# Square sums chained on VectorE, rows made k-tile by k-tile on ScalarE, and adaLN units loaded later: a hybrid decoder layer

## The chip, the core and the metric

One core of a Trainium2 chip runs the whole layer. The metric is the device time of one execution in microseconds, taken as the median of several runs. In the profile PE is TensorE (matrix products and transposes), ACT is ScalarE, DVE is VectorE, POOL is GpSimd, and SP (SyncE) issues the loads of the weights.

## What is computed

A layer on 256 tokens of width 1024, in fp32: a SwiGLU feed-forward part (ffn1), a token mixer (a causal pooling mixer and a dilated attention, from one input projection), and a second feed-forward part (ffn2). Each is preceded by an RMS norm whose result is scaled and shifted by vectors that are computed from a conditioning vector c (adaLN), and each result is multiplied by a gate vector from c and added to the running h.

```python
def rmsnorm(x, g):
    y = xf * lax.rsqrt(jnp.mean(xf * xf, axis=-1, keepdims=True) + EPS)
    return y * g
mod = silu(c) @ w_ada + b_ada                 # nine vectors of 1024
sh1, sc1, gt1, sh2, sc2, gt2, sh3, sc3, gt3 = split(mod, 9)
n = rmsnorm(h, g_ffn1) * (1 + sc1) + sh1
h = h + 0.5 * gt1 * swiglu(n, w1_gate, w1_up, w1_down)
n = rmsnorm(h, g_mix) * (1 + sc2) + sh2       # norm b
h = h + gt2 * hybrid_mixer(n, w_in, w_pool, pool_scale, w_out)
n = rmsnorm(h, g_ffn2) * (1 + sc3) + sh3      # norm c
h = h + 0.5 * gt3 * swiglu(n, w2_gate, w2_up, w2_down)
return rmsnorm(h, g_final)
```

## The kernel before

**Tiles and products.** The 256 tokens are two row tiles, t = 0 and t = 1, of 128 rows each. A width of 1024 is eight k-tiles of 128 columns. Every fp32 operand of a large product is split into a rounded part and a rest (nh and nl of an activation, hi and lo of a weight), and `gemm` adds three products, nh x hi, nl x hi and nh x lo, of 512 columns each, into a PSUM bank.

**Weights and adaLN.** Weights come through SP's queue as units of 1 MB, in the order that `plan` writes down, into four buffers (`raw`). A unit of weights is cast on ACT (hi, line 266) and subtracted on DVE (lo, line 267), in two halves of 1024 columns. A unit of kind `ada` is instead reduced on DVE by two operations of 1024 columns (line 255), which give two columns of `mod`. The function `weave` inserts these units among the weights; for the mixer the constant `WMIX` (line 42) says after which of its units they come. A buffer is loaded again when the DVE operations that read it are done.

**Order.** The tile scheduler orders every engine's instructions by priority and readiness. `urgent()` raises the priority of what stands in it, and `casts_after` with `behind` adds order dependencies that keep casts of later units behind given instructions.

**The norms between the stages.** Norm b lies between ffn1 and the mixer, norm c between the mixer's output projection (`wout`) and ffn2. For each row tile, `finish1` or `finish2` runs:
- `residual` (line 361): on DVE, two products of the accumulator and the gate row (line 364) and two sums into h (line 366), 512 columns each;
- `rstd` (line 289): two squares with a row sum on ACT (line 294); POOL adds the epsilon (line 296), adds both sums (line 298) and takes the power -1/2 (line 300);
- `norm_rows` (line 314): ACT multiplies both halves of the row by it (line 319, xs);
- later in PE's program, `norm_mod` (line 322): for each half PE transposes four blocks into PSUM (`turn`, line 307, xtb or xtc); then n32 = xs^T x scale + shift, per k-tile, on ACT for half 0 (line 336) and DVE for half 1 (line 338); then ACT casts 512 columns to nh (line 285) and DVE subtracts 512 columns to nl (line 286). In norm c the second half is only copied, and its k-tiles are finished one by one in ffn2.

**Where the turns stand.** Row tile 0's turn of norm b stands among the last four chunks of ffn1's second product for row tile 1, ahead of chunk number `TURN` (line 475). Row tile 1's turn stands in the mixer's second projection of row tile 0, ahead of k-tile 1 of `z["k0"]` (line 731); the turn of q0's heads stands at k-tile 3 there. The scores of the attention (`scores`) take a minimum on DVE (line 667), an exponential on ACT (line 669) and a scaling on DVE (line 673); `heads_out` transposes the probabilities on PE (line 681, pt), copies them on ACT (line 684, pts) and multiplies by the values on PE (line 690).

## Time and profile before

| | |
|---|---|
| median of 3 runs | 494.17 us (493.03 to 494.2) |
| the profiled execution | 494.21 us |
| span of its instructions | 492.4 us, so 1.8 us lie around it |
| mean granted TensorE clock | 0.993 |
| PE busy | 479.4 us (97%) |
| DVE busy | 354.8 us (72%) |
| ACT busy | 260.0 us (53%) |
| POOL busy | 15.6 us (3%) |

The profile gives one execution. A timeline row has the start, the duration and the instruction; in brackets stands how long its engine was idle before it, and what ended that. A row marked x4 groups four instructions. A matmul's start is the useful number, since matmuls overlap: at full clock one of 512 columns starts every 0.227 us. A window row gives, for a stretch, its length and each engine's busy time and count (PE, PE's weight loads, DVE, ACT, POOL), then the granted clock as a share of 2.4 GHz, the share of DMA time and GB/s.

### The profile page before, as it was taken

The page shows a single profiled execution, that of the slowest core. Times are in us where ns is not written, and L with a number is a line of the kernel's source. Part 1 is how long each engine was busy: PE and PEld are TensorE (multiplying, and loading weights), DVE is VectorE, ACT ScalarE, POOL GpSimd, SP SyncE. Part 2 cuts the span into 40 slices and gives each one's busy share as a digit, 9 for nine tenths or more (in the row PEclk, how much of TensorE's full clock was granted, in tenths as well). Part 3 has the DMA queues.
Part 4 walks back from the last instruction along what each step waited for, and adds up shares of the span by engine and source line. Part 5 has one row for each costly group of instructions (what it writes and reads, how often), then busy time and mean ns, then how long its engine had stood idle before and what let it go on. Part 6 is the DMA issues. An engine that isn't in the chain of part 4 may idle for free.

```text
span 492.4 us, 5990 instructions
## 1 busy us (share of the span) xinstructions
PE 479.4 (97%) x2176; PEld 385.1 (78%) x2176; DVE 354.8 (72%) x569; ACT 260.0 (53%) x437; POOL 15.6 (3%) x26
## 2 busy tenths in 40 slices
PE   8999999999999999899999999999999999999994
PEld 5778888888888887778767888888878888888883
DVE  5978989996897896787868776755666756655244
ACT  4776575553544354574677468945543443544121
POOL 1000000000000002120000012000000000000000
PEclk9999999999999999899999999999999999999998
DMA  8999995997987995859775848285367749540002
GB/s 306 400 359 315 369 338 203 369 425 281 396 325 286 338 385 193 309 198 405 317 244 184 298 154 318 106 321 197 126 236 253 281 189 341 180 162 9 35 2 85
DMA packets 20383, 126.05 MB, mean 256 GB/s; under 512 B 2409, under 2 KB 4225, under 8 KB 6018
## 3 DMA queue, kind: packets, MB, share of 16 engines
q1 hardware_dynamic: 17568, 121.25, 65.0%
q10 hardware_dynamic: 2786, 4.43, 2.6%
q8 instruction: 17, 0.28, 0.2%
q14 instruction: 12, 0.10, 0.1%
HBM read 124.61 MB, written 1.06 MB: 255 GB/s over the span
## 4 chain that ended last, share of the span: by engine, by line
PE 87%; DMA 5%; DVE 2%; ACT 2%; POOL 2%; issue 2%; POOLq 0%; DVEq 0%; ACTq 0%
PE accf L411 22%; PE gu L370 9%; PE le L445 9%; PE gu L371 9%; PE gu L372 9%; PE ld L445 6%; PE accm L762 5%; DMA raw<-in_w_dram 4%; PE zp L370 3%; PE zp L372 3%; PE zp L371 3%; PE ht L397 2%; DMA h<-in_x_dram 1%; ACT hi L266 1%; PE sh L370 1%
## 5 line engine op out<-in xcount | busy, mean ns | idle before, releaser
L267 DVE TENSOR_TENSOR lo<-raw,hi 128x1024 fp32r<-128x1024 f32 (+1 forms) x156 | 184.4, 1208 | 45.4 <-ACT hi L266 37.0
L266 ACT CAST hi<-raw 128x1024 fp32r<-128x1024 f32 (+1 forms) x156 | 158.3, 1041 | 78.9 <-PE accf L411 24.9
L255 DVE CUSTOM_DVE_ANT_0 raw<-raw,cb,vecs 128x1024 f32<-128x1024 f32 x70 | 88.1, 1279 | 4.8 <-DMA raw<-in_w_dram 4.8
L411 PE MATMUL accf<-hi,hh 128*128 128x512 f32 x176 | 56.3, 396 | 0.2
L411 PE MATMUL accf<-lo,hh 128*128 128x512 f32 x176 | 56.3, 394 | 0.0
L411 PE MATMUL accf<-hi,hl 128*128 128x512 f32 x176 | 55.7, 390 | 0.0
L370 PE MATMUL gu<-hi,nhc 128*128 128x512 f32 x112 | 44.4, 397 | 0.0
L372 PE MATMUL gu<-lo,nhc 128*128 128x512 f32 x112 | 43.7, 390 | 0.0
L371 PE MATMUL gu<-hi,nlc 128*128 128x512 f32 x112 | 43.7, 390 | 0.0
L388 ACT ACTIVATE sg<-gu 128x256 f32<-128x256 f32 x24 | 9.1, 381 | 65.2 <-PE gu L372 65.2
L411 PEld LDWEIGHTS accf<-hi,hl 128*128 128x128 f32 x176 | 33.0, 188 | 7.4 <-DVE hl L286 0.6
L411 PEld LDWEIGHTS accf<-lo,hh 128*128 128x128 f32 x176 | 33.3, 189 | 6.9
L411 PEld LDWEIGHTS accf<-hi,hh 128*128 128x128 f32 x176 | 32.7, 189 | 7.3 <-ACT hh L285 1.1
L391 DVE TENSOR_TENSOR pr<-sg,gu 128x256 f32<-128x256 f32 x24 | 10.0, 418 | 33.8 <-ACT sg L388 33.8
L370 PE MATMUL gu<-hi,nha 128*128 128x512 f32 x80 | 31.8, 397 | 0.0
L371 PE MATMUL gu<-hi,nla 128*128 128x512 f32 x80 | 31.2, 390 | 0.0
L372 PE MATMUL gu<-lo,nha 128*128 128x512 f32 x80 | 31.2, 390 | 0.0
L370 PE MATMUL zp<-hi,nhb 128*128 128x512 f32 x64 | 26.5, 416 | 0.0
L285 ACT CAST hh<-ht 128x256 fp32r<-128x256 f32 x44 | 14.1, 379 | 21.9 <-PE ht L397 21.9
L372 PE MATMUL zp<-lo,nhb 128*128 128x512 f32 x64 | 25.3, 395 | 0.0
L371 PE MATMUL zp<-hi,nlb 128*128 128x512 f32 x64 | 25.3, 395 | 0.0
L372 PEld LDWEIGHTS gu<-lo,nhc 128*128 128x128 f32 x112 | 21.0, 188 | 4.6
(172 smaller groups left out, 715.1 us busy)
## 6 DMA issues: line engine op xcount, KB each, us to landing
raw<-in_w_dram SPq DMA_DIRECT2D x112, 1024.0 KB, 5.1
raw<-in_w_dram SPq DMA_DIRECT2D x4, 512.0 KB, 7.7
gt<-gd ACTq DMA_DIRECT2D x3, 512.0 KB, 5.4
h<-in_x_dram SPq DMA_DIRECT2D x2, 512.0 KB
bias<-in_bias_dram ACTq DMA_DIRECT2D x4, 256.0 KB, 4.1
out_dram<-o SPq DMA_DIRECT2D x4, 160.0 KB, 2.1
bands<-in_band_dram ACTq DMA_DIRECT2D x4, 136.0 KB, 7.5
gfb<-in_gf_dram ACTq DMA_DIRECT2D x1, 512.0 KB, 4.8
```

Of the source, the lines that this page charges most:

```text
L255: note(nc.vector.tensor_tensor_reduce(r, r, cb, 1.0, vecs[:, m:m + 1], ALU.mult, ALU.add, mod[:, m:m + 1]), i, 1)
L266: note(nc.scalar.copy(hi[:, o:o + n], src), i + s / 2, 0)
L267: note(nc.vector.tensor_tensor(lo[:, o:o + n], src, hi[:, o:o + n].bitcast(F32), ALU.subtract), i + s / 2, 0)
L285: nc.scalar.copy(hi_ap, src)
L370: mm(ps, nh[:, k, :], whi, start=first, stop=False)
L371: mm(ps, nl[:, k, :], whi, start=False, stop=False)
L372: mm(ps, nh[:, k, :], wlo, start=False, stop=last)
L391: nc.vector.tensor_tensor(pr, sg, ps[:, 256:512], ALU.mult)
L397: nc.tensor.transpose(pt[:, i, :], pr[:, ts(i, P)], ident)
L411: mm(accs[b], a[:, k, :], cols(ww, 2 * k + b), start=st, stop=sp)
L445: mm(banks[ci][t], n[t][a][:, j, :], cols(ww, lead_set(f, j).index(ci)), start=j == 0 and p == 0, stop=last and p == 2)
L762: mm(acc2[t][b], a[:, k, :], cols(ww, 2 * kk + b), start=st, stop=sp)
```

## The change

`rstd` and `residual` are taken into `norm_rows`. The row's square sum is now two chained `tensor_tensor_reduce` on DVE, of which the first starts from the epsilon and the second from the first one's sum; POOL only takes the power. ACT makes half 0 of the scaled row and DVE half 1. In `norm_mod`, ACT makes both nh and n32 straight from PSUM, k-tile by k-tile, for both halves, and DVE subtracts two k-tiles at a time. `in_order` fixes the order of these on each engine, and `line_up` fixes in which order the rows, the casts of certain weight units and the k-tile operations come. `TURN` goes from 2 to 3, so that row tile 0's turn stands later in ffn1's chunks by program order; `AFTER1` moves row tile 1's turn from k-tile 1 to k-tile 3 of `z["k0"]`, and q0's heads turn at k-tile 5. `WMIX` loads the eight adaLN units of the mixer stage four weight units later.

```diff
-TURN = 2
+TURN = 3
+AFTER1 = 3
-WMIX = (0, 8)
+WMIX = (4, 12)
...
+    def in_order():
+        traced = nc.cur_bb.bb.instructions
+        done, last = len(traced), {}
+        yield last
+        for i in traced[done:]:
+            if i.engine in last:
+                order_dep(i, last[i.engine][1], "in order")
+            last[i.engine] = (last.get(i.engine, (i,))[0], i)
+    def line_up(*groups):
+        for (_, early), (late, _) in zip(groups, groups[1:]):
+            order_dep(late, early, "line up")
+    def halves_of(units, e):
+        return [(casts[u, s][e],) * 2 for u in units for s in range(2)]
...
-    def rstd(t, tag):
-        ss = tiny.tile([P, 2], F32, name=f"ss{tag}", tag="ss")
-        for b in range(2):
-            sq = work.tile([P, 512], F32, name=f"sq{tag}{b}", tag="t2", bufs=T2)
-            nc.scalar.activation(sq, h[:, t * D + b * 512:t * D + b * 512 + 512], AF.Square, accum_out=ss[:, b:b + 1])
-            if b == 0:
-                nc.gpsimd.tensor_tensor(ss[:, 0:1], ss[:, 0:1], deps, ALU.add)
-        v = tiny.tile([P, 1], F32, name=f"v{tag}", tag="v")
-        nc.gpsimd.tensor_tensor(v, ss[:, 0:1], ss[:, 1:2], ALU.add)
...
+    def norm_rows(t, tag, accs, g, units):
+        ss = None
+        for b in range(2):
+            tmp = work.tile([P, 512], F32, name=f"res{tag}{b}", tag="t2", bufs=T2)
+            nc.vector.tensor_tensor(tmp, accs[b], g[:, ts(b, 512)], ALU.mult)
+            hs = h[:, t * D + b * 512:t * D + b * 512 + 512]
+            nc.vector.tensor_tensor(hs, hs, tmp, ALU.add)
+            v = tiny.tile([P, 1], F32, name=f"v{tag}{b}", tag="v")
+            nc.vector.tensor_tensor_reduce(tmp, hs, hs, 1.0, D * EPS if ss is None else ss, ALU.mult, ALU.add, v)
+            ss = v
+        r = tiny.tile([P, 1], F32, name=f"r{tag}", tag="r")
+        nc.gpsimd.tensor_tensor(r, ss, mhalf, ALU.pow)
+        xs = [work.tile([P, 512], F32, name=f"xs{tag}{b}", tag="t2", bufs=T2) for b in range(2)]
+        rows = [nc.scalar.activation(xs[0], h[:, t * D:t * D + 512], AF.Copy, scale=r),
+                nc.vector.tensor_scalar(xs[1], h[:, t * D + 512:t * D + D], r, None, ALU.mult)]
+        casts_after([i.ins for i in rows], units)
...
-                    if b == 0:
-                        nc.scalar.activation(n32[:, i, :], pt[:, i, :], AF.Identity, bias=s, scale=a)
-                    else:
-                        nc.vector.tensor_scalar(n32[:, i, :], pt[:, i, :], a, s, ALU.mult, ALU.add)
-                split(nh[:, 4 * b:4 * b + 4, :], nl[:, 4 * b:4 * b + 4, :], n32)
+                    nc.scalar.activation(nh[:, j, :], pt[:, i, :], AF.Identity, bias=s, scale=a)
+                    nc.scalar.activation(n32[:, i, :], pt[:, i, :], AF.Identity, bias=s, scale=a)
+                    if i % 2:
+                        nc.vector.tensor_tensor(nl[:, j - 1:j + 1, :], n32[:, i - 1:i + 1, :],
+                                                nh[:, j - 1:j + 1, :].bitcast(F32), ALU.subtract)
...
+            xs = norm_rows(t, f"b{t}", nm["acc"][t], nm["g"],
+                           (place["win", (1, 1)] + 0.5 if t == 0 else place["win", (3, 0)], place["win", (1, 0)] + 1))
+        def after():
+            nm[t] = norm_mod(xs, 1, SH2, f"b{t}")
+            if t == 1:
+                r0, m0, r1, m1 = [chain[f"b{u}", kind] for u in range(NT) for kind in ("rows", "mod")]
+                soon = [halves_of([("win", (1, 1)), ("win", (2, 0))], e)[1:] for e in range(2)]
+                late = [halves_of([("win", (2, 1))], e) for e in range(2)]
+                line_up(r0[0], *soon[0], m0[0], *late[0], r1[0], m1[0])
+                line_up(r0[1], *soon[1], m0[1])
+                line_up(r1[1], *late[1], m1[1])
...
-    z["k0"] = zchunk(2, 0, 1.0, {1: after, 3: turn_heads("q0", qT, 0)})
+    z["k0"] = zchunk(2, 0, 1.0, {AFTER1: after, 5: turn_heads("q0", qT, 0)})
```

`finish2` is changed in the same way, with units of ffn2's lead in place of the mixer's.

The scheduler's result, first on PE around row tile 0's turn of norm b: accf is ffn1's accumulator of row tile 1, xtb the transposed rows. Before:

```order
846 L411 MATMUL accf_851<-lo_1_1449,hh_8_1_1504 128x512
847 L411 MATMUL accf_852<-lo_1_1449,hh_8_1_1504 128x512
848 L411 MATMUL accf_851<-hi_0_1470,hh_9_1_1608 128x512
849 L411 MATMUL accf_852<-hi_0_1470,hh_9_1_1608 128x512
850 L411 MATMUL accf_851<-hi_0_1470,hl_9_1_1609 128x512
851 L411 MATMUL accf_852<-hi_0_1470,hl_9_1_1609 128x512
852 L307 MATMUL xtb_1806<-ident,xsb_1776 128x128 x4
853 L411 MATMUL accf_851<-lo_0_1471,hh_9_1_1608 128x512
854 L307 MATMUL xtb_1818<-ident,xsb_1778 128x128 x4
```

And in the changed kernel:

```order
846 L428 MATMUL accf_851<-lo_1_1449,hh_8_1_1504 128x512
847 L316 MATMUL xtb_1798<-ident,xsb_1756 128x128 x4
848 L316 MATMUL xtb_1814<-ident,xsb_1757 128x128 x4
849 L428 MATMUL accf_852<-lo_1_1449,hh_8_1_1504 128x512
850 L428 MATMUL accf_851<-hi_0_1470,hh_9_1_1608 128x512
```

The first four transposes stand five rows earlier, and 25 products instead of 20 lie behind them ahead of the mixer's first product, which is row 874 in both.

On ACT, from row tile 0's row to row tile 1's row of norm b (sqb is the square, xsb the row, bias the loads of the attention's bias table). Before:

```order
161 L294 ACTIVATE sqb_1767,ssb_1766<-h 128x512
162 L294 ACTIVATE sqb_1770,ssb_1766<-h 128x512
163 L266 CAST hi_1_1677<-raw_1671 128x1024
164 L319 ACTIVATE xsb_1776<-h,rb_1774 128x512
165 L319 ACTIVATE xsb_1778<-h,rb_1774 128x512
166 L266 CAST hi_0_1699<-raw_1697 128x1024
167 L336 ACTIVATE n32b_1811<-xtb_1806,mod,acol 128x128 x4
168 L266 CAST hi_1_1703<-raw_1697 128x1024
169 L285 CAST nhb_1804<-n32b_1811 128x512
170 L285 CAST nhb_1804<-n32b_1823 128x512
```

And in the changed kernel, where eight pairs like rows 163 and 164 follow each other:

```order
159 L339 ACTIVATE xsb_1756<-h,rb_1754 128x512
160 L288 CAST hi_1_1647<-raw_1641 128x1024
161 L288 CAST hi_0_1665<-raw_1663 128x1024
162 L288 CAST hi_1_1669<-raw_1663 128x1024
163 L358 ACTIVATE nhb_1796<-xtb_1798,mod,acol 128x128
164 L359 ACTIVATE n32b_1803<-xtb_1798,mod,acol 128x128
```

Behind them, up to row tile 1's row and the first product's result z:

```order
181 L675 DMA bias_2297<-in_bias_dram 128x512
182 L675 DMA bias_2366<-in_bias_dram 128x512
183 L288 CAST hi_0_1687<-raw_1685 128x1024
184 L288 CAST hi_1_1691<-raw_1685 128x1024
185 L339 ACTIVATE xsb_1860<-h,rb_1858 128x512
186 L660 ACTIVATE z_1921<-zp_1868 128x512
```

The squares are gone, three casts stand between the row and the k-tile operations, and the four bias loads and two casts stand between those and the next row.

On DVE, from the residual of row tile 0 in the changed kernel (resb is the product with the gate, vb the square sum):

```order
235 L332 TENSOR_TENSOR h<-h,resb_1744 128x512
236 L332 TENSOR_TENSOR h<-h,resb_1749 128x512
237 L334 ISA resb_1744,vb_1747<-h 128x512
238 L334 ISA vb_1747 128x1
239 L334 ISA resb_1749,vb_1752<-h,vb_1747 128x512
240 L334 ISA vb_1752 128x1
241 L340 TENSOR_SCALAR xsb_1757<-h,rb_1754 128x512
242 L289 TENSOR_TENSOR lo_1_1648<-raw_1641,hi_1_1647 128x1024
```

Before, a weight subtraction (lo_1_1652) came right behind the second sum; now two square sums and half 1 of the row, which needs POOL's power, come ahead of it.

## Rows read from the trace of the kernel before

**Rows 1.** The page, part 4: shares of the chain that ended last, by engine.

```profile
PE 87%; DMA 5%; DVE 2%; ACT 2%; POOL 2%; issue 2%; POOLq 0%; DVEq 0%; ACTq 0%
```

**Rows 2.** Waits of PE over the whole span: total us, times, longest us.

```profile
PE xtb L307 <- ACT xsb L319: 3.1, 2, 2.5
```

**Rows 3.** PE timeline, norm of row tile 0: start, us, instruction, [idle <-releaser].

```profile
195.80 0.61 PE L411 MATMUL accf<-hi,hl 128*128 128x512 f32 x2
198.87 1.12 PE L307 MATMUL xtb<-ident,xsb 128*128 128x128 f32 x4 [2.46 <-ACT xsb L319]
...
202.25 0.63 PE L411 MATMUL accf<-hi,hl 128*128 128x512 f32 x2
...
205.89 0.61 PE L370 MATMUL zp<-hi,nhb 128*128 128x512 f32 x2
```

**Rows 4.** PE timeline, norm c of row tile 0.

```profile
294.34 1.03 PE L307 MATMUL xtc<-ident,xsc 128*128 128x128 f32 x8
...
295.68 0.62 PE L762 MATMUL accm<-hi,nly 128*128 128x512 f32 x2
```

**Rows 5.** Windows, norm of row tile 0: busy by engine, then PEclk, DMA share, GB/s.

```profile
199.00:200.00 1.00, 1.00 (x5) 1.00 (x6) 0.00 (x0) 1.00 (x2) 0.00 (x0) 0.50 0.69 221
...
203.00:204.00 1.00, 1.00 (x6) 0.84 (x5) 1.00 (x2) 0.75 (x2) 0.00 (x0) 1.00 1.03 426
```

**Rows 6.** Chain of waits, row tile 0: start, us, what.

```profile
192.37 1.06 ACT hi L266
193.43 0.63 ACT sqb L294 x2
...
194.19 1.19 POOL ssb L296
...
195.44 1.13 POOL vb L298
...
196.64 1.43 POOL rb L300
...
198.10 0.73 ACT xsb L319
```

**Rows 7.** DVE timeline: the residual of row tile 0.

```profile
190.56 1.29 DVE L364 TENSOR_TENSOR resa<-accf,gt 128x512 f32<-128x512 f32 x2 [1.13 <-PE accf L411]
191.76 1.28 DVE L366 TENSOR_TENSOR h<-h,resa 128x512 f32<-128x512 f32 x2
```

**Rows 8.** PE timeline, norm of row tile 1.

```profile
212.01 0.39 PE L370 MATMUL zp<-hi,nhb 128*128 128x512 f32 x1
213.05 1.27 PE L307 MATMUL xtb<-ident,xsb 128*128 128x128 f32 x8 [0.65 <-ACT xsb L319]
...
214.39 0.40 PE L372 MATMUL zp<-lo,nhb 128*128 128x512 f32 x1
```

**Rows 9.** Windows, norm of row tile 1.

```profile
213.00:215.00 2.00, 1.95 (x12) 1.62 (x13) 0.62 (x4) 2.00 (x5) 0.00 (x0) 1.00 0.72 213
```

**Rows 10.** Source lines 526, 667, 528: ns min/median/max of instructions akin to new ones.

```profile
L526 DVE CUSTOM_DVE_ANT_0 xs<-h x2: 1224/1225/1226, 4.7 to 6.3; 128x1024 f32<-128x1024 f32 x2
...
L667 DVE CUSTOM_DVE_ANT_0 p<-sc,bias x16: 269/354/421, 237.9 to 266.0; 128x128 f32<-128x128 f32 x8, 128x256 f32<-128x256 f32 x8
...
L528 POOL TENSOR_TENSOR rx<-vx,mhalf x2: 553/554/554, 6.1 to 7.6; 128x1 f32<-128x1 f32 x2
```

**Rows 11.** ACT timeline: four of the 128-column operations of norm_mod, row tile 1.

```profile
213.99 1.49 ACT L336 ACTIVATE n32b<-xtb,mod,acol 128x128 f32<-128x128 f32 x4
```

**Rows 12.** Source line 660: the four bias loads issued on ACT, ns.

```profile
L660 ACTq DMA_DIRECT2D bias<-in_bias_dram x4: 335/341/1027, 202.8 to 206.1; - x4
```

**Rows 13.** DVE timeline, residual of norm c, row tile 0.

```profile
286.60 1.29 DVE L364 TENSOR_TENSOR resm<-accm,gt 128x512 f32<-128x512 f32 x2 [0.95 <-PE accm L762]
```

**Rows 14.** Windows: attention, pooling and the head of wout.

```profile
236.00:284.00 48.00, 47.93 (x238) 34.87 (x238) 36.04 (x103) 29.66 (x76) 0.00 (x0) 1.00 0.69 256
```

**Rows 15.** Source line 690: waits of the product after the transposed probabilities.

```profile
  ACT pts L684: 1.4, 4
```

More of the change, by code (lines that the diff above doesn't have):

```diff
@@ L219, in block_kernel @@
     queues = {}
+    casts = {}
     done_mod = set()
@@ L267, in fetch @@
                 note(nc.vector.tensor_tensor(lo[:, o:o + n], src, hi[:, o:o + n].bitcast(F32), ALU.subtract), i + s / 2, 0)
+                casts[order[i], s] = bulk[-2][0].ins, bulk[-1][0].ins
             his.append(hi)
@@ L312, in new_n @@
                 npool.tile([P, KD, P], F32R, name=f"nl{tag}", tag="nl"))
-    def norm_rows(t, tag):
-        r = rstd(t, tag)
-        xs = []
+    chain = {}
+    def norm_rows(t, tag, accs, g, units):
+        ss = None
         for b in range(2):
-            xs.append(work.tile([P, 512], F32, name=f"xs{tag}{b}", tag="t2", bufs=T2))
-            nc.scalar.activation(xs[b], h[:, t * D + b * 512:t * D + b * 512 + 512], AF.Copy, scale=r)
+            tmp = work.tile([P, 512], F32, name=f"res{tag}{b}", tag="t2", bufs=T2)
[11 more added lines that the diff above has]
+        casts_after([i.ins for i in rows], units)
+        chain[tag, "rows"] = [(i.ins, i.ins) for i in rows]
         return xs
@@ L324, in norm_mod @@
         nh, nl = new_n(tag)
-        for b in range(2):
-            pt = turn(xs[b], f"xt{tag}{b}")
-            with urgent():
+        with urgent(), in_order() as last:
+            for b in range(2):
+                pt = turn(xs[b], f"xt{tag}{b}")
                 if xT is not None and b == 1:
@@ L359, in gate_rows @@
         return g
-    def residual(t, accs, g, tag):
-        for b in range(2):
-            tmp = work.tile([P, 512], F32, name=f"res{tag}{t}{b}", tag="t2", bufs=T2)
-            nc.vector.tensor_tensor(tmp, accs[b], g[:, ts(b, 512)], ALU.mult)
-            hs = h[:, t * D + b * 512:t * D + b * 512 + 512]
-            nc.vector.tensor_tensor(hs, hs, tmp, ALU.add)
     def gemm(ps, nh, nl, k, whi, wlo, first, last):
@@ L477, in ffn_rest @@
                 down(f, ci, 1, hid[ci][1], accs[1], banks)
-    @contextmanager
-    def in_order():
-        traced = nc.cur_bb.bb.instructions
-        done, last = len(traced), {}
-        yield last
-        for i in traced[done:]:
-            if i.engine in last:
-                order_dep(i, last[i.engine], "in order")
-            last[i.engine] = i
     spin_ps = accp.tile([P, 2 * P], F32, name="spin", tag="acc")
@@ L555, in block_kernel @@
             nc.vector.tensor_tensor(lo, src, hi.bitcast(F32), ALU.subtract)
-    casts_after([last[e] for e in last if e in (nc.scalar.engine, nc.vector.engine)], (2, 2))
+    casts_after([last[e][1] for e in last if e in (nc.scalar.engine, nc.vector.engine)], (2, 2))
     nm = {}
@@ L608, in finish1 @@
                 scale_cols(1, SC2)
-            residual(t, nm["acc"][t], nm["g"], "a")
-            xs = norm_rows(t, f"b{t}")
-        return lambda: nm.update({t: norm_mod(xs, 1, SH2, f"b{t}")})
+            xs = norm_rows(t, f"b{t}", nm["acc"][t], nm["g"],
[9 more added lines that the diff above has]
+                line_up(r1[1], *late[1], m1[1])
+        return after
     prs[2] = [second_half(2, t) for t in range(NT)]
@@ L769, in finish2, with after @@
                 scale_cols(2, SC3, 0, KD // 2)
-            residual(t, acc2[t], nm["g2"], "m")
-            xs = norm_rows(t, f"c{t}")
-        return lambda: n3.update({t: norm_mod(xs, 2, SH3, f"c{t}", t, xT3)})
+            xs = norm_rows(t, f"c{t}", acc2[t], nm["g2"],
+                           (place["lead", (1, 1)] + 0.5, place["lead", (1, 2)]) if t == 0 else
+                           (place["lead", (1, 4)], place["lead", (1, 2)]))
+        def after():
+            n3[t] = norm_mod(xs, 2, SH3, f"c{t}", t, xT3)
+            if t == 1:
+                r0, m0, r1, m1 = [chain[f"c{u}", kind] for u in range(NT) for kind in ("rows", "mod")]
+                soon = [halves_of([("lead", (1, 1)), ("lead", (1, 2))], e)[1:] for e in range(2)]
+                late = [halves_of([("lead", (1, 3))], e) for e in range(2)]
+                line_up(r0[0], *soon[0], m0[0], *late[0], r1[0], m1[0])
+                line_up(r0[1], *soon[1], m0[1])
+                line_up(r1[1], *late[1], m1[1])
+        return after
     wout(0, (0, 1))
```

5 lines of the change are left out of this document (2 added, 3 removed).

## The prediction

> **What bounds the kernel now.** Three views, in this order. The chain that ended last is 87% PE [rows 1]: the matmuls are the work, and only what keeps them waiting or slows them can be won. The table of waits then says where PE waits for this change's operations: twice in the whole span, 3.1 us, for the scaled rows xs on ACT [rows 2]. Last, the two places on PE's timeline.
>
> Row tile 0 (norm b, between ffn1 and the mixer): two matmuls start at 195.80, one every 0.227 us (sixteen from 202.25 to 205.89), so PE is at the transposes at 196.25; they start at 198.87 [rows 3]. That is 2.62 us of waiting. Then PE is slow. From 198.87 to 202.25 it does eight transposes and four matmuls; at norm c, where nothing waits, eight transposes and two matmuls take 295.68 - 294.34 = 1.34 us [rows 4], which makes 0.88 us for the eight, so the piece should take 0.88 + 0.91 = 1.79 and takes 3.38. The windows say why: the granted clock is 0.50 from 199 to 200, which is 1.2 GHz, and 1.00 (2.4 GHz) from 203 [rows 5]. So this norm costs 2.62 + 1.59 = 4.21 us.
>
> What ends late is read from the chain of waits [rows 6]: an ACT cast of weights that stands ahead of the squares (192.37), two squares, three POOL operations of 1.19, 1.13 and 1.43, and the row at 198.10. The residual itself starts at 190.56 and gives its last sum 2.4 us later (two products and two sums at 0.60 each) [rows 7].
>
> Row tile 1: the last matmul starts at 212.01, so PE is there at 212.24; the transposes start at 213.05 (0.81 us), and they and one matmul take 1.34 instead of 0.88 + 0.23 [rows 8]. This norm costs 1.04 us, with the clock at 1.00 all through [rows 9]. Norm c does not wait [rows 4].
>
> **The change, step by step** (times on the clock of the profile before).
>
> *Row tile 0, the row's scale.* Without the two squares on ACT, and with no ACT instruction between the sums and POOL, the chain is all DVE up to the power. In the PE order one matmul less stands ahead of the residual's last input, so it starts at 190.33; four operations of 0.60 end at 192.73. Two chained square sums of 128x512 have no row of this form: a 128x256 one takes 0.42 at most, a 128x1024 one 1.22 [rows 10]; I take 0.65 each, with the read and the wait of the second for the first, for 1.3 (bounds 1.0 and 2.4). That is 194.03. POOL's power is 0.55 where DVE did nothing heavy [rows 10] and 1.43 here, where DVE ran weight subtractions [rows 6]. I take 0.55: the next DVE instruction in the new order is the second half of the row, which itself waits for the power, so DVE is idle; the long row would cost 0.9 us more. The Trainium skill, "SBUF — State Buffer", section "SBUF: two separate sides", says that a DVE operation with two SBUF inputs and a GpSimd operation that reads SBUF lock each other out of a shared port pair; by it the power here is the short one and the sum stays. With 0.12 of handing over the power ends at 194.7, the row of half 0 (0.73 [rows 6]) at 195.45, and half 1 runs beside it on DVE and is wanted four transposes later.
>
> *Row tile 0, PE.* The transposes now stand five matmuls earlier, so PE is there at 195.12. It waits 0.33 by this working; I take 0.5 (up to 0.7). After a gap of 0.8 the clock did not fall [rows 8, 9], after 2.6 it did [rows 3, 5], so I take no fall. After that eight transposes and 25 matmuls: the mixer starts at 195.62 + 0.88 + 5.68 = 202.2 instead of 205.89. **Gain 3.7 us** (3.5 to 4.2).
>
> *Row tile 0, ACT and DVE behind the row.* ACT does three casts (1.0 each, to 198.5) and then sixteen 128-column operations, four of which take 1.49 [rows 11]: 6.0 us, to 204.5, in order of k-tiles. PE begins k-tile 0 at 202.2 and wants one k-tile in 0.68; its nl of k-tile 4 is wanted 16 matmuls in, at 205.8, and the DVE pair for it stands behind the first square sum of row tile 1, at about 205.6. Just in time: nothing counted.
>
> *Row tile 1.* The residual starts at 202.2, its square sum ends near 206.1 (four operations, two sums, one subtraction between), and the power at 206.7 to 207.6. ACT, in its order, still has four bias loads (three at 0.34, one at 1.03 [rows 12]) and two casts ahead of the row: 204.5 + 2.05 + 2.1 ends at 208.7, the row at 209.4. PE reaches these transposes 33 matmuls into the mixer instead of 28, at 209.7. **Gain 1.0 us** (0.7 to 1.04). The removed POOL additions and squares are on no other path.
>
> *Norm c, row tile 0.* Residual at 286.60 [rows 13], 2.4 of sums, 1.3 of square sums, 0.7 of power, 0.73 of row: 291.8. PE arrives ten matmuls earlier, at 292.07. Counted at nothing; if it were late by more than 0.3 it would be a new wait.
>
> *adaLN units loaded later.* Each is two DVE operations of 1.28 us. In the new DVE order thirteen of them, not seven, stand between the first score and norm c. DVE is busy 36.0 of 48 us there [rows 14], so 6 x 1.2 = 7.2 more fit into 12 idle ones; but DVE is in order, and some come between a score and its scaled probabilities. The product behind them waits for the transposed probabilities even now, four times for 1.4 us together [rows 15]: there is no slack at those places. Bounds: nothing, and 6 x 1.2 = 7.2 if each lies on the path. I take 0.6, about half of one. SP's queue keeps its number of loads; the mixer weights now come ahead of adaLN units, which only brings them earlier.
>
> *Sum:* 3.7 + 1.0 - 0.6 = 4.1 us. The profiled execution took 494.21, 0.04 above the median of the three runs (494.17), so **490.1 us**.
>
> **Rivals.**
> (a) *The mixer gives half of it back.* ACT now does sixteen operations per row tile where it did four, two casts and two squares, in an enforced order, and DVE the interleaved reductions. If nl of row tile 1 comes late because a reduction of an adaLN unit that has not landed stands ahead of its last pair, or the probabilities are late, PE loses 1.5 to 4 us: 491.6 to 494. For it: the margins above (0.2 us at k-tile 4). Against: DVE idles a quarter of the attention [rows 14].
> (b) *The clock falls all the same.* The wait of row tile 0 shrinks to 0.5 but 1.59 us at 1.2 GHz remain: 491.7. The Trainium skill, "TensorE: Matmul & The Clock Gate", Part 1, says that the gate follows how busy the engine was recently, so short gaps may add up. Against: the 0.8 us gap at row tile 1 with the clock at 1.00 [rows 9].
> (c) *Slower: the six reductions lie on the attention's path.* Each of them that stands between the maximum and the scaling of a head, with less slack than its own 1.2 us, holds the PE by the difference. It decides from five on the path: 5 x 1.2 = 6.0, and one clock fall of 1.59 as at row tile 0, 7.6 in all against 4.7 gained: 497.1. Against: in the order most lie between heads, and other matmuls (values, pooling input) are there to be run.
> (d) *No new stall at all*, and a wait of 0.3 at row tile 0: 3.9 + 1.04: 489.3.
> (e) *The chain is not shorter:* square sums at 1.2 each and a power of 1.43 make row tile 0 wait 2.4 us more than I take, the clock falls, and little is left: 494.
>
> **Numbers.** Forecast (489.4 to 491.4, with d) 0.60; (a) 0.20; (b) 0.08; (e) 0.05; (c) 0.07. A difference of 0.3% is about what a measurement here can tell: below 492.7 is faster, above 495.7 slower. Of (a) two thirds stay under 492.7; so faster 0.60 + 0.13 + 0.08 = 0.81, same 0.12, slower 0.07. The range from 488.9 (all bounds at their best: 4.2 + 1.04) to 493.4 takes in (b), (d) and most of (a).
>
> **What would show it.** Right: PE waits under 1 us for each xs, the granted clock stays at 1.00 from 196 to 204, POOL has one operation of 0.55 per norm, the mixer starts 3.7 us earlier and its last matmul 4.1 to 4.7 earlier. Wrong: a wait of PE for nl or nh of norm b, for pts or p, over 1 us; a window at 0.5 near 196; ACT's row of tile 1 ending after 209.7.

## The result

| | before | changed |
|---|---|---|
| median of 6 runs | 493.43 us (492.67 to 494.2) | 491.06 us (490.59 to 491.83) |
| ratio of the changed kernel to before | | 0.9941 (0.992 to 0.9962) |
| the profiled execution | 494.21 us, span 492.4 | 490.59 us, span 488.8 |

The change is faster by 0.59% (0.38 to 0.80), some 2.9 us where 4.1 were forecast; the medians lie 2.4 apart. The time lies in the stated range, 488.9 to 493.4. Of 51 executions of the kernel before that were timed beside the experiments, 31 had a mean granted clock of 0.993 to 0.995 and a median time of 494.17 us, and 20 had 0.996 or 0.997 and 492.63 us; the profiled one has 0.993.

The two profiled executions differ by 3.6 us, of which 0.9 stand before any norm: the first matmul of ffn1's last stretch is at 178.48 and 177.59, in an order that the change does not touch. To keep that out, the runs are compared by five stretches of PE's timeline, from matmul start to matmul start:

| stretch, us | before | changed | difference | forecast |
|---|---|---|---|---|
| A: ffn1's last stretch to the mixer's first matmul (norm b, tile 0) | 27.41 | 23.95 | -3.46 | -3.7 |
| B: to the first score (norm b, tile 1) | 29.87 | 28.76 | -1.11 | -1.0 |
| C: to the last matmul of wout (attention, norm c tile 0) | 61.96 | 63.36 | +1.40 | +0.6 |
| D: to the last matmul of ffn2's lead (norm c, tile 1) | 44.68 | 45.11 | +0.43 | 0 |
| E: to the last matmul | 142.47 | 142.38 | -0.09 | 0 |

The chain that ended last in the changed kernel, then PE's waits for rows (before: [rows 1], [rows 2]):

```profile
PE 90%; DMA 3%; DVE 3%; issue 2%; ACT 1%; POOL 0%; POOLq 0%; DVEq 0%
```

```profile
PE xtb L316 <- ACT xsb L339: 0.6, 1, 0.6
PE xtc L316 <- ACT xsc L339: 0.4, 1, 0.4
```

The wait for xsb has fallen from 3.1 us to 0.6, POOL's share of the chain from 2% to 0; a wait for xsc is new. Stretch A on PE, and a window behind the transposes (before: [rows 3], [rows 5]):

```profile
193.97 0.39 PE L428 MATMUL accf<-lo,hh 128*128 128x512 f32 x1
194.91 1.09 PE L316 MATMUL xtb<-ident,xsb 128*128 128x128 f32 x8 [0.56 <-ACT xsb L339]
...
201.54 0.39 PE L387 MATMUL zp<-hi,nhb 128*128 128x512 f32 x1
```

```profile
199.00:200.00 1.00, 1.00 (x6) 0.81 (x6) 0.66 (x2) 1.00 (x4) 0.00 (x0) 1.00 0.90 377
```

PE waits 0.71 us from the natural start (193.97 + 0.23) to 194.91, and the clock stays at 1.00 in every window from 192 to 201, where it fell to 0.50 before. What releases it, on DVE and POOL (before: [rows 6], [rows 7]):

```profile
189.41 1.29 DVE L330 TENSOR_TENSOR resb<-accf,gt 128x512 f32<-128x512 f32 x2 [2.07 <-PE accf L428]
...
191.82 0.68 DVE L334 CUSTOM_DVE_ANT_0 resb<-h 128x512 f32<-128x512 f32 x1
...
192.65 0.75 DVE L334 CUSTOM_DVE_ANT_0 resb<-h,vb 128x512 f32<-128x512 f32 x1
...
194.14 0.49 DVE L340 TENSOR_SCALAR xsb<-h,rb 128x512 f32<-128x512 f32 x1 [0.73 <-POOL rb L337]
```

```profile
193.56 0.55 POOL L337 TENSOR_TENSOR rb<-vb,mhalf 128x1 f32<-128x1 f32 x1 [185.31 <-DVE vb L334]
```

The two square sums take 0.68 and 0.75, from 191.82 to 193.4; POOL's one operation takes 0.55 and half 1 of the row starts right behind it. Row tile 1 comes without a wait, because ACT's row ends at 207.12, 1.9 us before PE's transposes start (before: [rows 8]). PE, then ACT:

```profile
209.06 1.03 PE L316 MATMUL xtb<-ident,xsb 128*128 128x128 f32 x8
```

```profile
206.40 0.72 ACT L339 ACTIVATE xsb<-h,rb 128x512 f32<-128x512 f32 x1 [1.24 <-POOL rb L337]
```

Stretch C: DVE is busy 40.5 of 48 us where it was 36.0 ([rows 14]); its columns are those of that group.

```profile
236.00:284.00 48.00, 47.98 (x234) 34.97 (x233) 40.54 (x101) 28.17 (x68) 0.00 (x0) 1.00 0.80 300
```

No wait that this could cause stands in PE's table of waits. What has changed is where the attention's products stand on PE. `heads_out` multiplies the probabilities of two heads, a pair, into the two halves of one tile yt, two products for each head (of 256 and of 128 columns). There are four pairs. In the kernel before, three of them stand together on PE and one is split; in the changed kernel one stands together, and in three pairs scores (sc), matmuls of the projections (zp, accm) or the second head's transposes (pt) come between the heads. A split pair of the changed kernel (sc and zp, which stand between, are left out), and a pair together, in experiment 6 below:

```profile
258.22 0.65 PE L705 MATMUL yt<-pts,z 128*64 128x256 f32 x2
258.80 0.44 PE L696 MATMUL pt<-ident,p 128*128 128x128 f32 x2
259.17 0.43 PE L706 MATMUL yt<-pts,z 128*64 128x128 f32 x2
...
260.80 0.65 PE L705 MATMUL yt<-pts,z 128*64 128x256 f32 x2
261.29 0.38 PE L706 MATMUL yt<-pts,z 128*64 128x128 f32 x2
```

```profile
258.74 0.66 PE L706 MATMUL yt<-pts,z 128*64 128x256 f32 x4
259.22 0.39 PE L707 MATMUL yt<-pts,z 128*64 128x128 f32 x4
```

The second head alone takes 0.80 us, from 260.80 to the next start at 261.60; both heads together take as long, 258.74 to 259.54. (In other places, where the records stand in the order 256, 128, 256, 128, they take 1.02 to 1.30.) So the products of the two heads run side by side where nothing stands between them. A split pair costs 0.99 us by experiments 11 and 12. From start to next start, 0.48 us of this in experiment 11 and 0.78 in experiment 12 lie at the products themselves; the rest lies at the transposes and scores that stood between or beside them.

Stretch D: the transposes of norm c's row tile 1 now stand 21 matmuls into ffn2's lead, not 36, and wait for the row that ACT makes at 298.48:

```profile
298.42 0.39 PE L462 MATMUL le<-lo,nhc 128*128 128x512 f32 x1
299.26 1.09 PE L316 MATMUL xtc<-ident,xsc 128*128 128x128 f32 x8 [0.45 <-ACT xsc L339]
```

```profile
298.48 0.72 ACT L339 ACTIVATE xsc<-h,rc 128x512 f32<-128x512 f32 x1 [2.30 <-POOL rc L337]
```

From 298.42 to 299.26 are 0.84 us, of which 0.23 are the matmul's own: 0.61 lost, in a norm that waited for nothing before.

### The profile page after: what moved, and what is told of

Read it like the earlier page. It is cut to its first block, busy times and chain, and to the rows that moved or that the text cites. A ratio compares the mean times of both kernels' runs of the same rounds, so it can differ in the third digit from the quotient of the medians.

```text
span 488.8 us, 5989 instructions
## 1 busy us (share of the span) xinstructions
PE 478.0 (98%) x2176; PEld 383.6 (78%) x2176; DVE 358.9 (73%) x587; ACT 260.1 (53%) x443; POOL 5.9 (1%) x18
## 3 DMA queue, kind: packets, MB, share of 16 engines
HBM read 124.61 MB, written 1.06 MB: 257 GB/s over the span
## 4 chain that ended last, share of the span: by engine, by line
PE 90%; DMA 3%; DVE 3%; issue 2%; ACT 1%; POOL 0%; POOLq 0%; DVEq 0%
PE accf L428 21%; PE gu L387 9%; PE gu L389 9%; PE gu L388 9%; PE ld L462 8%; PE le L462 8%; PE accm L777 5%; PE zp L387 3%; PE zp L389 3%; PE zp L388 3%; DMA raw<-in_w_dram 3%; PE ht L414 2%; PE yt L705 1%; DMA h<-in_x_dram 1%; PE sh L389 1%
## 5 line engine op out<-in xcount | busy, mean ns | idle before, releaser
L309 DVE TENSOR_TENSOR hl<-ht,hh 128x256 fp32r<-128x256 f32 x44 | 16.4, 416 | 14.4 <-ACT hh L308 14.4
```

Source lines behind the costliest of these rows:

```text
L309: nc.vector.tensor_tensor(lo_ap, src, hi_ap.bitcast(F32), ALU.subtract)
```

## The experiments

Ratios are to the kernel before, measured on the same chip; the changed kernel's is 0.9941. The stretches of all, the number of split pairs, PE's waits in stretch C, and what is left of C after 0.99 us for each split pair and the waits (this rest still varies, from 59.75 to 60.97, and that is not explained):

| run | ratio (95%) | A | B | C | D | split | waits in C | rest of C |
|---|---|---|---|---|---|---|---|---|
| before | 1 | 27.41 | 29.87 | 61.96 | 44.68 | 1 | 0 | 60.97 |
| changed | 0.9941 (0.992 to 0.9962) | 23.95 | 28.76 | 63.36 | 45.11 | 3 | 0 | 60.39 |
| 1, units early | 0.9941 (0.9926 to 0.9956) | 24.03 | 29.51 | 62.18 | 45.12 | 2 | 0.45 | 59.75 |
| 2, turns not urgent | 0.9932 (0.9917 to 0.9947) | 23.24 | 28.97 | 63.29 | 44.41 | 2 | 0.55 | 60.76 |
| 3, rows alone | 0.9982 (0.9967 to 0.9997) | 24.62 | 29.43 | 63.14 | 46.19 | 2 | 0.80 | 60.36 |
| 4, squares on ACT | 0.9955 (0.9941 to 0.9969) | 23.98 | 28.75 | 63.11 | 45.18 | 1 | 1.42 | 60.70 |
| 5, order alone | 0.9954 (0.9937 to 0.9971) | 23.32 | 30.70 | 61.58 | 46.20 | 1 | 0 | 60.59 |
| 6, not urgent, units (3, 11) | 0.9881 (0.9861 to 0.9901) | 23.24 | 28.99 | 61.65 | 44.45 | 1 | 0 | 60.66 |
| 7, not urgent, units early, row first | 0.9883 (0.9863 to 0.9903) | 23.23 | 28.91 | 61.56 | 44.41 | 1 | 0 | 60.57 |
| 8, no line-up | 0.9928 (0.9910 to 0.9946) | 24.00 | 29.70 | 61.11 | 45.73 | 1 | 0 | 60.12 |
| 9, ACT's order only | 1.0010 (0.9991 to 1.0029) | 25.03 | 32.67 | 61.30 | 45.20 | 1 | 0 | 60.31 |
| 10, DVE's order only | 0.9927 (0.9906 to 0.9949) | 23.27 | 30.06 | 61.55 | 44.72 | 1 | 0 | 60.56 |
| 11, pairs together | 0.9887 (0.9868 to 0.9906) | 24.02 | 28.79 | 60.38 | 45.09 | 0 | 0 | 60.38 |
| 12, experiment 7 with pairs together | 0.9859 (0.9844 to 0.9873) | 23.17 | 28.92 | 60.57 | 44.41 | 0 | 0 | 60.57 |

### What shortened the row's chain

**Experiment 3** puts the chained square sums into the kernel before.

```diff
 def rstd(t, tag):
-    # (two squares on ACT, two additions on POOL)
+        nc.vector.tensor_tensor_reduce(tmp, hs, hs, 1.0, D * EPS if ss is None else ss, ALU.mult, ALU.add, v)
     # (the power on POOL stays)
 def norm_rows(t, tag):
+    # half 1 of the row:
+    nc.vector.tensor_scalar(xs[1], ..., r, None, ALU.mult)
```

> The kernel before with the chained square sums on DVE and half 1 of the row on DVE, and nothing else: norm_mod, the places of the turns and the adaLN units as before. My theory: this part alone takes the waits for xs (2.62 and 0.81 us) and the clock fall (1.6 us) away; the mixer's first matmul comes 3.4 to 4.2 us earlier, less up to 1 us by which the old 512-column casts and subtractions now end after PE wants them. Time 1.5 to 4 us below before (ratio 0.992 to 0.997). Rival, the k-tile operations carry the gain: PE waits 2 us or more for nl at the mixer's first matmuls, the clock falls there, and the time is within 0.8 us of before.

Only 0.9982, some 0.9 us: less than the 1.5 to 4 us that were expected. The chain is there, but in the scheduler's order weight subtractions stand between its parts on DVE, and beside the power. DVE, POOL, and PE's waits:

```profile
192.94 1.22 DVE L267 TENSOR_TENSOR lo<-raw,hi 128x1024 fp32r<-128x1024 f32 x1
194.08 0.74 DVE L296 CUSTOM_DVE_ANT_0 sqb<-h,vb 128x512 f32<-128x512 f32 x1
...
194.75 1.22 DVE L267 TENSOR_TENSOR lo<-raw,hi 128x1024 fp32r<-128x1024 f32 x1
```

```profile
194.98 1.40 POOL L299 TENSOR_TENSOR rb<-vb,mhalf 128x1 f32<-128x1 f32 x1 [186.39 <-DVE vb L296]
```

```profile
PE xtb L306 <- ACT xsb L319: 1.7, 2, 1.2
PE le L447 <- DVE nlc L286: 1.4, 1, 1.4
...
PE xtc L306 <- ACT xsc L319: 0.8, 1, 0.8
```

The power takes 1.40 beside a weight subtraction, not 0.55; the subtraction ahead of the second sum adds 1.14. PE waits for both norms' rows, and 1.4 us for nl of norm c. The long wait for nl at the mixer, by which the rival had it, did not come.

**Experiment 4** leaves the change as it is and puts the squares back on ACT and the additions on POOL.

```diff
-            nc.vector.tensor_tensor_reduce(tmp, hs, hs, 1.0, D * EPS if ss is None else ss, ALU.mult, ALU.add, v)
+            nc.scalar.activation(t2, sq[b], AF.Square, accum_out=ss[:, b:b + 1])
+            # (and the two nc.gpsimd.tensor_tensor additions, as before)
```

> The changed kernel with the squares on ACT and the two additions on POOL as before; the k-tile operations, the order constraints, the turns and the adaLN units as changed. My theory: the three POOL operations and the squares put 2 to 3 us back into the chain; PE waits 2 to 3.5 us at norm b row tile 0 with the clock at 0.50 for 2 to 3 us behind it, and 0.5 us or more at the other norms: 3.5 to 6 us above the changed kernel, so not faster than before. Rival, the order of casts and rows is what counted, not the chain: the wait is under 1.2 us, no window at 0.50, and the time within 1.5 us of the changed kernel.

My theory fell: stretch A is 23.98, as in the changed kernel. POOL's three operations take 0.19, 0.19 and 0.55 where they took 1.19, 1.13 and 1.43 [rows 6], and the transposes start as early:

```profile
192.66 0.19 POOL L339 TENSOR_TENSOR ssb<-ssb,deps 128x1 f32<-128x1 f32 x1 [184.48 <-ACT sqb L337]
193.27 0.19 POOL L341 TENSOR_TENSOR vb<-ssb 128x1 f32<-128x1 f32 x1 [0.42 <-ACT sqb L337]
193.54 0.55 POOL L343 TENSOR_TENSOR rb<-vb,mhalf 128x1 f32<-128x1 f32 x1
```

```profile
194.90 1.10 PE L316 MATMUL xtb<-ident,xsb 128*128 128x128 f32 x8 [0.53 <-ACT xsb L345]
```

From the residual's start to ACT's row it takes 4.25 us (189.87 to 194.12), in the changed kernel 4.73 (189.41 to 194.14): the engine of the squares is not what counts here. (At row tile 0 of norm c it may: the squares start at 283.91, behind another ACT operation of 1.06 us, the same chain takes 5.19 us against 4.63, and PE waits 1.03 us for the row, where the changed kernel waits for none.) The new theory: nothing else may run on DVE while POOL works. **Experiment 5** adds only that, and the same for ACT, to the kernel before.

```diff
+            if b == 0: rows = [nc.scalar.activation(xs[b], ..., AF.Copy, scale=r)]
+            else: rows.append(nc.vector.tensor_scalar(xs[b], ..., r, None, ALU.mult))
+        casts_after([i.ins for i in rows], units)
```

> The kernel before with one thing: the casts and subtractions of the mixer's and the lead's weights are kept behind the rows (the changed kernel's casts_after), and half 1 of the row is made on DVE so that DVE too has an instruction to keep them behind. The squares stay on ACT, the two additions on POOL, the 512-column norm_mod, the turns and the adaLN units as before. Theory now: the chain to the row was long because a cast stood ahead of the squares on ACT and weight subtractions ran on DVE beside POOL's operations, not because of the engine that squares; so POOL's three operations take under 0.3, 0.3 and 0.7 us here instead of 1.18, 1.12 and 1.42, PE waits under 0.8 us for the row at norm b row tile 0, no window there is at 0.50, and the stretch from the first matmul behind the last FFN chunk to the mixer's first matmul goes from 27.41 to 23.6 to 24.8 us; time 1.5 to 3.5 us below before. Rival, the chained squares on DVE are needed: POOL stays above 1 us each or the wait above 1.5 us, and the stretch above 26.

Stretch A is 23.32 us, shorter than in the changed kernel; the transposes start at 194.84 without a wait. It loses elsewhere: PE waits 0.7 and 0.8 us for z in the mixer (stretch B) and 1.0 for nl of norm c (stretch D). The changed kernel has none of these waits; which of its other parts (k-tile operations, places of the turns, line-up) avoids them was not tested. **Experiments 9 and 10** part the two orders: 9 keeps both halves of the row on ACT and holds back only ACT's casts, 10 holds back only DVE's subtractions.

```diff
 9:  casts_after([rows[0].ins], units)      both halves on ACT
10:  casts_after([rows[1].ins], units)      half 1 on DVE
```

> The kernel before with the weight casts on ACT kept behind the first half of the row; both halves of the row stay on ACT, so nothing holds DVE back (the fifth experiment without its DVE half). DVE then runs adaLN reductions or weight subtractions beside POOL. Theory: POOL's operations are slow because of DVE's work beside them, so they take about 1.1, 1.1 and 1.4 us again here (0.19, 0.19 and 0.55 in the fifth experiment), the row comes about 1.5 to 2.5 us later than there and PE waits 1.2 to 2.5 us for it at norm b row tile 0. Rival, the cast ahead of the squares was the whole delay: PE waits under 0.7 us and POOL takes under 0.7 us each.

> The kernel before with half 1 of the row on DVE and the weight subtractions kept behind it; ACT is not held back, so one cast stands ahead of the squares and one between the squares and the row. Theory: POOL takes 0.19, 0.19 and 0.55 us because DVE waits, and the two casts cost 0.5 to 1.6 us of the chain: PE waits 0.4 to 1.8 us at norm b row tile 0, less than in the experiment with ACT's order alone. Rival, the casts count as much as DVE's work: PE waits 2 us or more.

In experiment 9 adaLN reductions run on DVE beside POOL. POOL, DVE, PE, and two windows:

```profile
193.17 0.94 POOL L296 TENSOR_TENSOR ssb<-ssb,deps 128x1 f32<-128x1 f32 x1 [184.80 <-ACT sqb L294]
194.19 1.13 POOL L298 TENSOR_TENSOR vb<-ssb 128x1 f32<-128x1 f32 x1
```

```profile
192.79 1.27 DVE L255 CUSTOM_DVE_ANT_0 raw<-raw,cb,vecs 128x1024 f32<-128x1024 f32 x1
...
193.99 1.28 DVE L255 CUSTOM_DVE_ANT_0 raw<-raw,cb,vecs 128x1024 f32<-128x1024 f32 x1
```

```profile
194.71 0.61 PE L415 MATMUL accf<-lo,hh 128*128 128x512 f32 x2
196.76 1.27 PE L307 MATMUL xtb<-ident,xsb 128*128 128x128 f32 x8 [1.43 <-ACT xsb L320]
...
209.23 0.39 PE L376 MATMUL zp<-lo,nhb 128*128 128x512 f32 x1
211.53 1.71 PE L307 MATMUL xtb<-ident,xsb 128*128 128x128 f32 x8 [1.90 <-ACT xsb L320]
```

```profile
198.00:200.00 2.00, 2.00 (x11) 1.61 (x10) 1.71 (x3) 2.00 (x6) 0.00 (x0) 1.00 0.77 320
212.00:214.00 2.00, 2.00 (x9) 1.67 (x8) 0.66 (x3) 2.00 (x7) 0.00 (x0) 0.55 1.05 397
```

POOL is at 0.94 and 1.13 (its power, when DVE has nothing left to run, at 0.55), and PE waits 1.6 us (195.16 to 196.76) and 2.1 us (209.46 to 211.53) for the two rows; nothing is won. In experiment 10, with a cast of 1.06 ahead of the squares still there, POOL and PE:

```profile
193.16 0.19 POOL L296 TENSOR_TENSOR ssb<-ssb,deps 128x1 f32<-128x1 f32 x1 [184.92 <-ACT sqb L294]
193.78 0.19 POOL L298 TENSOR_TENSOR vb<-ssb 128x1 f32<-128x1 f32 x1 [0.42 <-ACT sqb L294]
194.05 0.55 POOL L300 TENSOR_TENSOR rb<-vb,mhalf 128x1 f32<-128x1 f32 x1
```

```profile
195.41 1.09 PE L307 MATMUL xtb<-ident,xsb 128*128 128x128 f32 x8
```

POOL is at 0.19, 0.19 and 0.55, and there is no wait at all for a row, at 0.9927: this one order, with the half row on DVE that it needs, does as much for the time as the whole change. (Experiment 3 has the half row on DVE without the order, and its power is at 1.40. My 0.4 to 1.8 us of waiting was too much: the cast ahead of the squares ended, at 192.11, before the first sum did.)

### What was given back, and versions that keep it

**Experiment 2** takes the transposes out of the raised priority.

```diff
-        with urgent(), in_order() as last:
+        with in_order() as last:
             for b in range(2):
                 pt = turn(xs[b], f"xt{tag}{b}")
+                with urgent():
```

> The changed kernel with the transposes of the rows outside the raised priority, as before; the ACT and DVE operations behind them keep it. They stand 13 matmuls later for row tile 0 of norm b, 5 later for row tile 1, 11 and 14 later in norm c. My theory: PE waits for xs at norm b row tile 0 (0.71 us in the changed kernel's matmul starts) and at norm c row tile 1 (0.61) only because the transposes come too early; both waits go, the operations behind are still in time, and the time falls by 0.9 to 1.4 us against the changed kernel. Rival: the k-tile operations on ACT (6 us for a row tile) are then late and PE waits for nh or nl at the first mixer matmuls and at ffn2's first ones by 0.5 us or more each: no gain or a loss.

As expected in A and D (0.71 and 0.70 less, no wait for a row is left). Stretch C stays at 63.29: one split pair less, but a wait of 0.55 for the transposed probabilities (pts), the only one over 0.1 us in any run. By the ratios the time falls by 0.4 us, where 0.9 to 1.4 were expected.

**Experiment 1** undoes the later adaLN units.

```diff
-WMIX = (4, 12)
+WMIX = (0, 8)
```

> The changed kernel with the adaLN units of the mixer stage loaded as before (WMIX (0, 8)); all else as changed. My theory: the two norms b gain about 4.5 us, and 1.4 us of that is given back between the first score and the end of wout (61.96 us from first score to last wout matmul before, 63.36 changed), because of the order in which PE's probability transposes and their products come, not because of the reductions: that stretch stays at 62.8 to 63.6 and the time within 0.5 us of the changed kernel. Rival 1, late reductions on DVE hold the probabilities: the stretch falls to 62.0 to 62.4 and the time by 1.0 to 1.4 us against the changed kernel (ratio to before about 0.992). Rival 2, loading late is what keeps row tile 1 free: PE waits over 0.5 us for nl or nh of norm b and the time rises by 0.5 to 2 us.

C falls by 1.2, with one split pair less, although a new wait of 0.45 for norm c's row 0 is in it; but B rises by 0.75, and the time stays. My theory had C at 62.8 or more; 62.18 is what the rival, late reductions, had. Experiments 11 and 12 decide between the two, against the rival. ACT's two casts wait for the third mixer unit's weights until 207.2, and row tile 1's row stands behind them:

```profile
207.20 2.00 ACT L288 CAST hi<-raw 128x1024 fp32r<-128x1024 f32 x2 [3.61 <-DMA raw<-in_w_dram]
...
209.10 0.71 ACT L339 ACTIVATE xsb<-h,rb 128x512 f32<-128x512 f32 x1
```

**Experiments 6 and 7** combine: 6 is experiment 2 with the units one place earlier, 7 is experiment 2 with the units as before and row tile 1's row ahead of those casts.

```diff
6: -WMIX = (4, 12)
   +WMIX = (3, 11)
7: +WMIX = (0, 8)
   -    line_up(r0[0], *soon[0], m0[0], *late[0], r1[0], m1[0])
   +    line_up(r0[0], *soon[0], m0[0], r1[0], *late[0], m1[0])
```

> The changed kernel with the transposes of the rows outside the raised priority (as the second experiment) and the mixer's adaLN units one place earlier (WMIX (3, 11)). In PE's order no probability transpose is then directly followed by the product of the other head's, except at the end. Theory: what the changed kernel lost in the attention (63.36 against 61.96 us from first score to last wout matmul) is PE's order there, which the place of the adaLN units moves; the stretch falls to 61.6 to 62.6 and the time 0.5 to 1.5 us below that of the second experiment (489.4), ratio to before 0.990 to 0.993. Rival: the stretch stays above 63 and the time within 0.4 us of the second experiment.

> The changed kernel with the transposes outside the raised priority, the adaLN units loaded as before (WMIX (0, 8)), and row tile 1's row of norm b ahead of the two casts of the third mixer unit on ACT instead of behind them. Theory: in the first experiment the units' early load let those casts wait 3.6 us for their weights, and the row stood behind them; with the row ahead of them the stretch from the mixer's first matmul to the first score falls from 29.51 to 28.6 to 29.0, the attention stretch is 61.8 to 62.6, and the time is 488.4 to 489.3. Rival: the casts behind the row are then late for the mixer's own matmuls and PE waits 0.5 us or more for the third unit's hi or lo.

Both hold, and win more than was expected: C is 61.65 and 61.56, A, B and D are the shortest or nearly so, and the ratios, 0.9881 and 0.9883, lie below the changed kernel's interval. Both have one split pair where the changed kernel has three. In experiment 7 no row, nh, nl, pts or z is waited for any more; PE's whole table of waits is the start of the program:

```profile
PE spin L503 <- POOL ident masks.py:199: 1.4, 1, 1.4
PE ld L463 <- ACT nha L442: 0.8, 1, 0.8
```

**Experiment 8** removes the line-up.

```diff
-                line_up(
+                0 and line_up(      # all six calls
```

> The changed kernel without line_up (casts_after and in_order stay). On ACT one cast instead of three then stands between row tile 0's row and its k-tile operations, on DVE the scheduler is free. Theory: the line-up only shifts which of two works in time comes first; PE's waits at norm b stay within 0.4 us of the changed kernel's, and the time within 0.8 us of it. Rival, the line-up is what holds the weight casts in time or the k-tile operations together: PE waits over 1 us for nl, hi or lo in the mixer and the time rises by 1 to 3 us.

0.9928, within the expected 0.8 us of the changed kernel, but not for the expected reason: PE waits 1.3 us for rows of norm b in place of 0.6, and 1.1 in place of 0.4 for norm c, and C is 61.11, with one split pair.

So far the split pairs were only read from PE's order in runs that differ in other things too. **Experiments 11 and 12** add one order for that: the first product of a pair is not scheduled ahead of the copy of the second head's probabilities, in the changed kernel (11) and in experiment 7 (12).

```diff
-                nc.scalar.copy(sb, pt.rearrange("p a b -> p (a b)"))
+                done = nc.scalar.copy(sb, pt.rearrange("p a b -> p (a b)"))
-            mm(ps[o, :], v[0][:, ts(hd, DH)], pts[e][:, 0:S], start=True, stop=False)
+            first = mm(ps[o, :], v[0][:, ts(hd, DH)], pts[e][:, 0:S], start=True, stop=False)
+            if e == 0:
+                order_dep(first.ins, done.ins, "pair")
```

> The changed kernel, with one order added: the first head's product with its probabilities is not scheduled before the copy of the second head's transposed probabilities, so that the four products of a pair of heads stand together on PE. In the changed kernel three of the four pairs are split, in the kernel before one, in experiments 6 and 7 one. Theory (a split pair costs its second head's products, about 0.8 to 1.0 us, because two heads' products beside each other take 0.80 us together and one head's alone 0.80 too): stretch C falls from 63.4 to 60.4 to 61.0, A, B and D stay, and the ratio comes to about 0.988 (0.986 to 0.990). Rival (the adaLN reductions on DVE lie on the attention's path, and the split order only fills a wait that is there anyway): PE then waits at the products, pts or p, for 1 to 3 us, and C stays at 62.5 or more, ratio 0.992 to 0.995.

> Experiment 7 (transposes not urgent, adaLN units as before, row of tile 1 ahead of the late casts) with the same order added: its one split pair stands together too. Theory of the split pairs: stretch C from 61.56 to about 60.6 (60.3 to 61.0), the rest as in experiment 7, ratio 0.9863 (0.985 to 0.9875). Rival (the split filled a wait): C stays at 61.2 to 61.8, with a wait of PE for pts of up to 1 us, ratio 0.988 to 0.9895.

C falls by 2.98 for three pairs and by 0.99 for one; A, B and D stay within 0.07, and no wait for pts or p comes in. So there was no wait to be filled, and each split cost 0.99 us. Nor do the reductions on DVE lengthen C: without split pairs it is 60.38 with the units late (13 reduction operations in it) and 60.57 with them early (8). The third pair of experiment 11, whose products take 1.25 us together, from 259.52 to the next start at 260.77:

```profile
259.52 0.89 PE L705 MATMUL yt<-pts,z 128*64 128x256 f32 x3
...
260.46 0.38 PE L708 MATMUL yt<-pts,z 128*64 128x128 f32 x2
```

0.9859 is the best of all: 1.41% below the kernel before, where the change has 0.59.

## Why the prediction was right, and where not

**Row tile 0: the size held, the reason only in part.** The forecast was a wait of 0.5, no clock fall and 3.7 us; it is 0.71, no window at 0.50, and 3.46. The square sums took 1.6 us with their reads (191.82 to 193.41, I took 1.3 by a reading of other forms), the power 0.55 as forecast, and the step "the next DVE instruction in the new order is the second half of the row, which itself waits for the power, so DVE is idle" names what the runs then showed to be the cause. But I costed it as a gain of 0.9 on one operation and put the rest down to the removed squares and additions. Experiments 4 and 10 show that these cost nothing at this place where DVE waits: three POOL operations take 0.93 us together, not 3.75, and the chain from the residual's start to the row is 4.25 us with the squares on ACT and 4.73 with the sums on DVE (7.54 before). The sums were no part of the gain there. The 0.55 itself was read from a place where DVE was not idle: it starts an operation of 1.23 us at 6.28, 0.16 us behind the first power of [rows 10]. The number held all the same, and the last section says why. The Trainium skill, "SBUF — State Buffer", section "SBUF: two separate sides", says that a DVE operation with two SBUF inputs and a GpSimd operation that reads SBUF exclude each other for a whole instruction; the runs agree where the DVE operation is under way first, 0.19 against 0.94 to 1.19 for the same addition, and not where POOL's starts first (last section).

Of the 3.7 us, 1.59 were the clock fall, and I took it as paid in every execution. The granted clocks in the section on the result say otherwise: the two groups of executions lie 1.54 us apart, the price of one fall, so in all likelihood some 31 of 51 have it. An estimate from these counts is that its removal is worth 0.9 us on average, not 1.59.

**Row tile 1** gained 1.11 where 1.0 was forecast. The row ended at 207.12, where I had 209.4, because the bias loads did not hold ACT up: they were issued beside its k-tile operations, the first at 199.13 and the last at 201.73, and those ran without a gap from 197.60 to 203.3.

**Stretch C, the later adaLN units,** is the term that was mis-sized: "I take 0.6, about half of one", and the stretch lost 1.40. The mechanism was also another one. I looked for a wait of PE for the probabilities, because DVE is busier; there is none over 0.1 us, and by experiments 11 and 12 the reductions cost nothing there. I had also misread [rows 15]: its four waits are those of PE's weight loads (PEld), which overlap the matmuls, as the table of waits of the kernel before says:

```profile
PEld yt L690 <- ACT pts L684: 1.4, 4, 0.4
```

PE itself waited 0.07 us there. The loss is in the order that the scheduler gives PE: two more split pairs, 2 x 0.99, less 0.6 that the rest of the stretch won (60.97 to 60.39 in the table). By start to next start, the products take 1.27 us more and the transposes of the probabilities 0.71, the mixer's projections 0.70 less; why these won I have not traced. That the place of the units alone decides which pairs are split is not shown: with the units where they stood before, two pairs are split in experiments 1 and 3, and with them later one in experiment 4. Why the scheduler splits them is open as well.

**Norm c** was "counted at nothing", and I had worked out row tile 0 only. There it held, no wait. At row tile 1 the transposes come 15 matmuls earlier in PE's order, which I had not looked up, and lose 0.61; experiment 2 gets it back.

**The sum.** The five stretches as measured sum to 2.83 us, near the 0.59% of the runs. That is in part luck, because the profiled execution of the kernel before has the clock fall and many others have not. The last matmul is 3.7 us earlier, 2.8 without the start of the program, where I had named 4.1 to 4.7; the other signs of being right held or nearly so, and none of being wrong came.

Of the rivals, (a) was the nearest: part of the gain is given back beside the mixer, but in PE's order, not in a wait for nl or probabilities. (b) did not come about, nor did (c), (d) and (e).

## What to carry to other kernels

Before a chain is moved to another engine, see what runs beside it: POOL's additions cost up to six times as much when they start behind DVE's two-input operations, and one ordering constraint that kept DVE waiting was worth as much as the rewrite. Raising the priority of an instruction that PE executes moves the wait onto PE; raise that of what feeds it, and leave the transposes where the row is ready. Where a scheduler sets the order, look for operations that are cheap only beside each other: a stretch can lose microseconds with no wait in the profile, and start to start over whole stretches shows it. Before the price of a clock fall is put into a forecast, look at the granted clocks of many executions and not of the profiled one alone.

## What the runs showed of the hardware that was not expected

Four products of two heads that fill the two halves of one tile take 0.80 to 1.30 us together, and two of one head 0.80: the two heads' products overlap when nothing stands between them. The Trainium skill, "TensorE: Matmul & The Clock Gate", Part 3, says that matmuls that use only a part of the array can run in it at the same time; the trace agrees, and shows that the scheduler's order can undo it.

What lengthens an operation on POOL is a two-input DVE operation that is under way when it starts; one that starts behind it did not. In the kernel before, the power of norm c's row tile 0 starts 0.08 us ahead of a subtraction (POOL, DVE):

```profile
291.83 0.55 POOL L300 TENSOR_TENSOR rc<-vc,mhalf 128x1 f32<-128x1 f32 x1
291.91 1.23 DVE L267 TENSOR_TENSOR lo<-raw,hi 128x1024 fp32r<-128x1024 f32 x1 [0.47 <-ACT hi L266]
```

The power takes 0.55, and the subtraction 1.23, as long as elsewhere (1.22 in the rows of experiment 3). With a subtraction under way the power takes 1.40 to 1.43 (experiment 3, [rows 6]).

Whether TensorE's clock falls behind a wait differs from execution to execution. In the profiles it stayed at 2.4 GHz (1.00) behind a wait of 1.6 us (experiment 9, row tile 0), and fell to 1.2 GHz behind one of 2.1 us (experiment 9, row tile 1, 0.55 from 212 to 214) and one of 2.62 (before, 0.50). But seven of the ten executions of experiment 9 have a mean granted clock of 0.992 or 0.993 and three have 0.995 or 0.996, and the kernel before parts in the same way, 31 to 20. The profiles show one execution each, so that the others had no fall is read from these means alone. The price of a fall should be given a chance.
